# Down projection of two ConvFFNs: a chunk's norm is issued inside the next chunk

## Chip, cores and metric

The kernel runs on one core of one Trainium2 chip. The metric is device time in microseconds, the median of the runs. All times below come from the runs, from one profiled execution, or are worked out from its rows.

## The reference, cut to what matters

Two layers, each a mixer and a ConvFFN, on 1040 tokens (16 learned ones and 1024 given ones) of width 1024. Each sub-layer is wrapped in two RMS norms:

```
for i in range(2):
    h = h + rms_norm(mixer_i(rms_norm(h, pre)), post)
    h = h + rms_norm(conv_ffn(rms_norm(h, f_pre), w_up, c_w, c_b, w_down), f_post)
return h[:, 16:]

def conv_ffn(u, w_up, conv_w, conv_b, w_down):       # w_up 1024 x 5632, w_down 2816 x 1024
    h = causal_dwconv(u @ w_up, conv_w, conv_b)      # 3 taps
    g, up = split(h, 2)
    return (gelu(g) * up) @ w_down
```

The mixer of layer 0 is a gated linear recurrence beside a sliding-window attention, that of layer 1 a chunked state-space scan; both end in an output projection (2048 x 1024).

## The kernel before

Activations lie transposed, with the feature on the partitions and the tokens along the free dimension, in three chunks of tokens (348, 346 and 346 columns in layer 0; 342 each in layer 1, the first one of the last ConvFFN cut to 340). A product of two float32 values is made of three float32r matmuls: each operand is split into a high part (a ScalarE copy that rounds) and a low part (VectorE: value minus high part), and `mm3` issues high x high, high x low and low x high (L236, L237, L238).

**Weights.** `Weights` keeps one list of all weight tiles of the program in order of use. SyncE loads a tile of 128x1024 into `wst` (3 buffers), ScalarE and VectorE split it (`whi` L107, `wlo` L108) into two of the 8 buffers `w8`, so that at most four split tiles are alive. `get` hands out the next tile and issues the splits of the two after it.

**Down projection** (second half of `ffn`). For each chunk: load the 22 tiles of the gated product from DRAM (`mr`, L475) through the shared buffers `hc` (7 of them), split them into `mh` (L478) and `ml` (L479); then two halves `mb` of four output tiles each, and within a half 11 weight tiles. A weight tile serves two of the 22 tiles and four outputs, 24 matmuls. The four outputs of a half end together, go from PSUM to `yc` (L494, one buffer for the chunk) and are squared (`SqSum.add`). There are 6 PSUM banks for outputs, and 2 (`pb`) for the norms. Then the chunk's norm follows.

**Norm** (`norm_chunk`). It loads 8 tiles of the old `h` into `hc`. GpSimd has added up the 8 squares; 6 small matmuls (`pst`, L166) sum over the partitions, VectorE adds epsilon, GpSimd raises to -1/2, 6 small matmuls (`rb`, L180) spread the result over the partitions. Then for each of 8 tiles: VectorE multiplies `yc` by the norm's weight and by `rb` (`pt`, L205), GpSimd (VectorE for tiles 0 and 4, and for all in the last sub-layer) adds it to `h` (L207), and in layer 0's ConvFFN ScalarE and VectorE write the high and low part of the next sub-layer's input (L216, L217). Squares for the next norm are added up likewise.

**Up projection.** After three plain tiles the rest is multiplied by a seven-product scheme on halves of each operand. Its right-hand factors T1, T2, T4 (`right_factors`) and T3 (`third_factor`) are made once per layer from tiles `b` loaded from DRAM; T3 overwrites a part of `uh`/`ul` that the plain tiles read before. The subtractions of T2, T4 and T3 (L375, L377, L384) are GpSimd's, that of T1 is VectorE's. `right_factors` takes six `hc` buffers for each of its 8 steps. Results leave PSUM through `xs` (L334).

**Order.** The framework orders each engine's instructions when the program is built, by a simulated time line (`schedule_with_timeline_sim=True`): an engine takes the instruction that stands first in the program among those that are ready in that time line. On the chip each engine then follows that order.

The functions are printed with the profile's line numbers:

Of the kernel before, what the change touches and what calls it, by code (L numbers as in the profile page):

```python
# [13 lines left out]
F32 = mybir.dt.float32  # L14
# [125 lines left out]
class SqSum:  # L140
# [3 lines left out]
    def __init__(self, k, n, name):  # L144
        self.k, self.n, self.name, self.acc = k, n, name, None

    def add(self, src, m):
        k, nc, n = self.k, self.k.nc, self.n
        if self.acc is not None:
# [4 lines left out]
        if sq is not self.acc:  # L154
# [30 lines left out]
def norm_chunk(k, c, acc, y_of, h_src, h_dst, w_post, w_pre, name, between=lambda m: None, u_dst=None,  # L185
               more=None):
# [13 lines left out]
    if w_pre is not None:  # L200
        acc2 = SqSum(k, n, "h" + name)
    for m in range(NK):
        if y_of is not None:
            t = k.work.tile([P, NMAX], F32, tag="pt", bufs=2, name=f"pt_{name}_{m}")
            nc.vector.scalar_tensor_tensor(t[:, :n], y_of(m), w_post[:, m:m + 1], rb[:, :n], ALU.mult, ALU.mult)  # L205
            eng = nc.vector if m % 4 == 0 or w_pre is None else nc.gpsimd
            eng.tensor_tensor(h[m][:, :n], h[m][:, :n], t[:, :n], ALU.add)  # L207
        if h_dst is not None:
            nc.sync.dma_start(h_dst(m, t0, n), h[m][:, :n])
        if w_pre is None:  # L210
            continue
        if u_dst is not None:
            acc2.add(h[m][:, :n], m)
            continue
        hi, lo = k.uh[:, m, t0:t0 + n], k.ul[:, m, t0:t0 + n]
        nc.scalar.activation(hi, h[m][:, :n], AF.Copy, scale=w_pre[:, m:m + 1])  # L216
        nc.vector.scalar_tensor_tensor(lo, h[m][:, :n], w_pre[:, m:m + 1], hi.bitcast(F32), ALU.mult, ALU.subtract)  # L217
        if y_of is not None or m >= 4:
            for j in (range(m + 1) if y_of is None and m == 4 else (m,)):
                acc2.add(h[j][:, :n], j)  # L220
# [69 lines left out]
def ffn(k, W, lay, chunks, out_lo, conv_w, conv_b, ud, md, norm):  # L290
# [7 lines left out]
    with ExitStack() as es:  # L298
# [62 lines left out]
        def quarter(nm, s, kk):  # L361
            t0, n, _ = HALF[lay][s]
            b = k.work.tile([P, NMAX], F32, tag="hc", bufs=7, name=f"{nm}_{lay}_{s}_{kk}")[:, :n]
# [101 lines left out]
    with ExitStack() as es:  # L465
        ypool = es.enter_context(tc.tile_pool(name=f"ffy{lay}", bufs=1, reuse_waits="tile"))
        pool = es.enter_context(tc.tile_pool(name=f"ffd{lay}", bufs=1, side="right", reuse_waits="tile"))
        pp = es.enter_context(tc.tile_pool(name=f"ffdps{lay}", bufs=6, space=PSUM, reuse_waits="tile"))
        for ci, (t0, n) in enumerate(chunks):
            o = max(out_lo - t0, 0)  # L470
            t0, n = t0 + o, n - o
            mid = []
            for i in range(NFF):
                r = k.work.tile([P, NMAX], F32, tag="hc", bufs=7, name=f"mr{lay}_{ci}_{i}")
                nc.sync.dma_start(r[:, :n], md[i][:, t0:t0 + n])  # L475
                h = pool.tile([P, NMAX], F32R, tag="mh", bufs=NFF, name=f"mh{lay}_{ci}_{i}")
                l = pool.tile([P, NMAX], F32R, tag="ml", bufs=NFF, name=f"ml{lay}_{ci}_{i}")
                nc.scalar.copy(h[:, :n], r[:, :n])  # L478
                nc.vector.tensor_tensor(l[:, :n], r[:, :n], h[:, :n].bitcast(F32), ALU.subtract)  # L479
                mid.append((h, l))  # L480
            yc = ypool.tile([P, NK, NMAX], F32, tag="yc", bufs=1, name=f"fy{lay}_{ci}")
            acc = SqSum(k, n, f"y{lay}_{ci}")
            for mb in (0, 1):
                ps = [pp.tile([P, 512], F32, tag="ps", name=f"dn{lay}_{ci}_{mb}_{q}") for q in range(4)]
                for i in range(NFF):
                    if i % 2 == 0:
                        w = W.get("dn", lay, ci, mb, i // 2)
                    h, l = mid[i]
                    for q in range(4):
                        s = slice((i % 2) * 512 + q * P, (i % 2) * 512 + (q + 1) * P)  # L490
                        mm3(nc, ps[q][:, :n], w[0][:, s], w[1][:, s], h[:, :n], l[:, :n], i == 0, i == NFF - 1)
                for q in range(4):
                    m = mb * 4 + q
                    nc.scalar.copy(yc[:, m, :n], ps[q][:, :n])  # L494
                    acc.add(yc[:, m, :n], m)
            norm((t0, n), acc, lambda m: yc[:, m, :n], f"f{lay}_{ci}")
# [38 lines left out]
def out_proj(k, W, zd, chunks, norm, lay):  # L535
# [5 lines left out]
    with ExitStack() as es:  # L541
# [4 lines left out]
        for ci, (t0, n) in enumerate(chunks):  # L546
# [10 lines left out]
            acc = SqSum(k, n, f"o{lay}_{ci}")  # L557
# [27 lines left out]
            norm((t0, n), acc, lambda m: yc[:, m, :n], f"o{lay}_{ci}", (pool, "zr", 4))  # L585
# [656 lines left out]
def build(tc, I, O):  # L1242
# [16 lines left out]
    with ExitStack() as es:  # L1259
# [29 lines left out]
        def norm(s):  # L1289
            def f(c, acc, y_of, name, more=None):  # L1290
# [5 lines left out]
                           u_dst=None if s % 2 else lambda m, t0, n: ud[m][:, t0:t0 + n], more=more)  # L1296
# [40 lines left out]
```

## Time and profile before

| what | value |
|---|---|
| median of 3 runs | 3317.67 us (3315.75 to 3318.92) |
| the profiled execution's own time | 3317.06 us |
| its span, first to last instruction | 3315.3 us |
| outside the span | 1.8 us |
| TensorE busy | 3160.7 us, 95% |
| mean granted TensorE clock | 0.976 |

TensorE is busy for most of the span, so what counts is where it is not, and where it runs at the lower of its two clock levels (granted clock 0.50).

### The profile page before, as it was taken

How to read it: one execution, taken by the hardware profiler on the slowest of the kernel's cores; microseconds unless marked ns; L12 is line 12 of the kernel's file. 1: busy time of each engine (PE TensorE's matmuls, PEld its weight loads, DVE VectorE, ACT ScalarE, POOL GpSimd, SP SyncE). 2: the span in 40 equal slices, each digit the busy share in tenths (PEclk: the TensorE clock that was granted, in tenths of full speed). 3: DMA queues.
4: the chain of work that ended last, by engine and by line, in shares of the span. 5: the costliest groups of instructions: out<-in, count | busy, mean ns of one | idle time of the engine just before them, and what ended most of it. 6: DMA issues, size and time to landing. Idle time of an engine off the chain costs nothing.

```text
span 3315.3 us, 55448 instructions
## 1 busy us (share of the span) xinstructions
PE 3160.7 (95%) x21424; PEld 3046.8 (92%) x21424; DVE 2114.8 (64%) x3877; ACT 1609.7 (49%) x2920; POOL 539.7 (16%) x902
## 2 busy tenths in 40 slices
PE   8999999999999998989999999999999999999888
PEld 8888887999999998989999999999999999999888
DVE  6654344556888873455786667765565888885443
ACT  6763455554544453444554444444454544544332
POOL 3110000335000001123121111111244400000000
PEclk9999999999999999989999999999999999999889
DMA  3211013664222244553111111111575422225553
GB/s 127 80 64 59 29 36 115 202 222 138 88 84 78 78 159 138 185 181 99 37 44 45 37 50 53 41 43 45 193 225 175 125 81 82 81 83 183 188 172 106
DMA packets 165481, 352.59 MB, mean 106 GB/s; under 512 B 20032, under 2 KB 99808, under 8 KB 165216
## 3 DMA queue, kind: packets, MB, share of 16 engines
q1 hardware_dynamic: 165216, 349.04, 32.4%
q8 instruction: 168, 2.75, 0.3%
q14 instruction: 97, 0.79, 0.1%
HBM read 282.78 MB, written 65.59 MB: 105 GB/s over the span
## 4 chain that ended last, share of the span: by engine, by line
PE 83%; DVE 4%; ACT 4%; DMA 3%; issue 3%; POOL 2%; SPq 0%; POOLq 0%; DVEq 0%; ACTq 0%
PE ps_g L236 6%; PE ps_g L238 6%; PE ps_g L237 6%; PE upS L236 5%; PE upS L237 5%; PE upS L238 5%; PE dn L237 5%; PE dn L238 5%; PE dn L236 5%; PE op L238 2%; PE op L237 2%; PE op L236 2%; PE upA L236 2%; DMA zr<-zd 2%; PE upA L237 2%
## 5 line engine op out<-in xcount | busy, mean ns | idle before, releaser
L108 DVE TENSOR_TENSOR wlo<-wst,whi 128x1024 fp32r<-128x1024 f32 x318 | 394.7, 1244 | 401.3 <-ACT whi L107 383.4
L107 ACT CAST whi<-wst 128x1024 fp32r<-128x1024 f32 x319 | 332.9, 1046 | 460.6 <-PE dn L237 234.8
L238 PE MATMUL ps_g<-uh,wlo 128*128 128x346 f32 (+2 forms) x1344 | 442.3, 329 | 0.6 <-DVE wlo L108 0.6
L236 PE MATMUL ps_g<-uh,whi 128*128 128x346 f32 (+2 forms) x1344 | 440.3, 328 | 0.6 <-DVE dtr L945 0.4
L237 PE MATMUL ps_g<-ul,whi 128*128 128x346 f32 (+2 forms) x1344 | 440.2, 328 | 0.0
L236 PE MATMUL dn<-mh,whi 128*128 128x346 f32 (+3 forms) x1056 | 339.0, 329 | 47.3 <-ACT mh L478 47.3
L237 PE MATMUL dn<-ml,whi 128*128 128x346 f32 (+3 forms) x1056 | 344.6, 326 | 2.9 <-DVE ml L479 2.9
L238 PE MATMUL dn<-mh,wlo 128*128 128x346 f32 (+3 forms) x1056 | 342.3, 325 | 0.0
L236 PEld LDWEIGHTS ps_g<-uh,whi 128*128 128x128 f32 x1344 | 253.8, 189 | 6.1 <-DVE dtr L945 0.7
L238 PEld LDWEIGHTS ps_g<-uh,wlo 128*128 128x128 f32 x1344 | 253.8, 189 | 5.3 <-DVE wlo L108 1.1
L237 PEld LDWEIGHTS ps_g<-ul,whi 128*128 128x128 f32 x1344 | 253.8, 189 | 4.2 <-issue 0.2
L238 PE MATMUL op<-zh,wlo 128*128 128x342 f32 (+2 forms) x768 | 248.6, 324 | 2.5 <-DVE wlo L108 2.3
L237 PE MATMUL op<-zl,whi 128*128 128x342 f32 (+2 forms) x768 | 249.6, 326 | 0.9 <-DVE zl L555 0.9
L236 PE MATMUL op<-zh,whi 128*128 128x342 f32 (+2 forms) x768 | 244.9, 326 | 4.5 <-ACT zh L554 4.0
L236 PEld LDWEIGHTS dn<-mh,whi 128*128 128x128 f32 x1056 | 203.0, 194 | 48.8 <-ACT mh L478 48.8
L237 PEld LDWEIGHTS dn<-ml,whi 128*128 128x128 f32 x1056 | 203.3, 193 | 4.7 <-DVE ml L479 4.7
L238 PEld LDWEIGHTS dn<-mh,wlo 128*128 128x128 f32 x1056 | 203.5, 193 | 0.0
L82 ACT CAST wb<-wst 128x512 fp32r<-128x512 f32 x228 | 141.0, 618 | 102.2 <-PE upS L238 94.1
L83 DVE TENSOR_TENSOR wb<-wst,wb 128x512 fp32r<-128x512 f32 x228 | 156.2, 686 | 25.6 <-ACT wb L82 25.6
L236 PE MATMUL upA<-uh,wb 128*128 128x260 f32 (+2 forms) x608 | 171.8, 283 | 0.0
L236 PE MATMUL upS<-uh,wb 128*128 128x260 f32 (+2 forms) x608 | 171.6, 282 | 0.0
L237 PE MATMUL upA<-ul,wb 128*128 128x260 f32 (+2 forms) x608 | 171.3, 282 | 0.0
(430 smaller groups left out, 8693.7 us busy)
## 6 DMA issues: line engine op xcount, KB each, us to landing
wst<-in_dn SPq DMA_DIRECT2D x132, 512.0 KB, 3.5
wst<-in_wo SPq DMA_DIRECT2D x96, 512.0 KB, 3.9
wst<-in_up SPq DMA_DIRECT2D x88, 512.0 KB, 3.5
wst<-in_w SPq DMA_DIRECT2D x74, 512.0 KB, 3.5
md<-cv_u SPq DMA_DIRECT2D x38, 260.0 KB, 2.1
zd<-x SPq DMA_DIRECT2D x16, 513.0 KB, 3.5
zr<-zd SPq DMA_DIRECT2D x48, 171.0 KB, 3.2
mr<-md SPq DMA_DIRECT2D x44, 173.0 KB, 3.3
```

What stands on the lines that cost most here:

```text
L82: nc.scalar.copy(p[:, 0], src)
L83: tt(p[:, 1], src, p[:, 0].bitcast(F32), ALU.subtract)
L107: nc.scalar.copy(h, s)
L108: nc.vector.tensor_tensor(l, s, h.bitcast(F32), ALU.subtract)
L236: nc.tensor.matmul(ps, lhsT=wh, rhs=xh, start=start, stop=False, skip_group_check=more)
L237: nc.tensor.matmul(ps, lhsT=wh, rhs=xl, start=False, stop=False, skip_group_check=more)
L238: nc.tensor.matmul(ps, lhsT=wl, rhs=xh, start=False, stop=stop, skip_group_check=more)
```

## The change

The norm of a chunk of the down projection is kept as a closure (`before`) and issued after the first half `mb` of the next chunk; the last chunk's norm follows after the loop. The split tiles (`mid`, high and low part in one tile) move from a pool on the right side of SBUF to the pool that holds `yc`, on the left side, where the factors T1, T2 and T4 of the up projection lay before; there are still 22. In each half the last weight tile is used output by output, so that the four outputs end one after the other.

For the last chunk of every sub-layer (`tail`, `last`) the squares are not added up by GpSimd: each square goes straight into 6 small matmuls that accumulate over the 8 tiles (`direct`). There, six of the eight additions to `h` are VectorE's and two GpSimd's (tiles 2 and 5).

In the up projection the subtractions of T2, T4 and T3 move from GpSimd to VectorE, and three of the six buffers of a step are taken from the norms' buffers `acc`, `sq` and `pt` in place of `hc`.

```diff
+    def __init__(self, k, n, name, direct=False):
+        self.first = True
+        if direct:
+            self.pst = k.pb.tile([P, 512], F32, tag="pb", name=f"pst_{name}")
     def add(self, src, m):
         nc.scalar.activation(sq[:, :n], src, AF.Square)
+        if self.direct:
+            nb, w, st = token_blocks(n)
+            for j in range(nb):
+                nc.tensor.matmul(self.pst[:w, j:j + 1], lhsT=sq[:, st[j]:st[j] + w], rhs=k.mean_d, start=self.first,
+                                 stop=m == NK - 1, skip_group_check=True)
+                self.first = False
     def rsqrt(self, name):
+        if self.direct:
+            return rsqrt_rows(self.k, self.pst, self.n, name)
...
+            if last:
+                eng = nc.gpsimd if m in (2, 5) else nc.vector
+            else:
+                eng = nc.vector if m % 4 == 0 or w_pre is None else nc.gpsimd
...
+            tag, bufs = {"b21": ("acc", 2), "t1": ("sq", 2), "t2": ("pt", 2)}.get(nm, ("hc", 7))
...
-                nc.gpsimd.tensor_tensor(t2, b22, t1, ALU.subtract)
+                nc.vector.tensor_tensor(t2, b22, t1, ALU.subtract)
-                nc.gpsimd.tensor_tensor(b21, b21, t2, ALU.subtract)
+                nc.vector.tensor_tensor(b21, b21, t2, ALU.subtract)
...
-                nc.gpsimd.tensor_tensor(b12, b22, b12, ALU.subtract)
+                nc.vector.tensor_tensor(b12, b22, b12, ALU.subtract)
...
-        pool = es.enter_context(tc.tile_pool(name=f"ffd{lay}", bufs=1, side="right", reuse_waits="tile"))
+        before = None
+            tail = ci == len(chunks) - 1
-                h = pool.tile([P, NMAX], F32R, tag="mh", bufs=NFF, name=f"mh{lay}_{ci}_{i}")
-                l = pool.tile([P, NMAX], F32R, tag="ml", bufs=NFF, name=f"ml{lay}_{ci}_{i}")
+                x = ypool.tile([P, 2, NMAX], F32R, tag="mid", bufs=NFF, name=f"mid{lay}_{ci}_{i}")
+                h, l = x[:, 0, :n], x[:, 1, :n]
...
+            def part(m, js):
+                for i in js:
+                    w = ws[i // 2]
+                    s = slice((i % 2) * 512 + m % 4 * P, (i % 2) * 512 + (m % 4 + 1) * P)
+                    mm3(nc, ps[m][:, :n], w[0][:, s], w[1][:, s], *mid[i], i == 0, i == NFF - 1)
+            for mb in (0, 1):
+                ms = range(mb * 4, mb * 4 + 4)
+                for m in ms:
+                    ps[m] = pp.tile([P, 512], F32, tag="ps", name=f"dn{lay}_{ci}_{m}")
+                for i in range(0, NFF - 2, 2):
+                    ws[i // 2] = W.get("dn", lay, ci, mb, i // 2)
+                    for m in ms:
+                        part(m, (i, i + 1))
+                ws[NFF // 2 - 1] = W.get("dn", lay, ci, mb, NFF // 2 - 1)
+                for m in ms:
+                    part(m, (NFF - 2, NFF - 1))
+                if mb == 0:
+                    if before:
+                        before()
+                    yc = ypool.tile([P, NK, NMAX], F32, tag="yc", bufs=1, name=f"fy{lay}_{ci}")
+                    acc = SqSum(k, n, f"y{lay}_{ci}", tail)
+                for m in ms:
+                    nc.scalar.copy(yc[:, m, :n], ps[m][:, :n])
+                    acc.add(yc[:, m, :n], m)
-            norm((t0, n), acc, lambda m: yc[:, m, :n], f"f{lay}_{ci}")
+            def before(c=(t0, n), acc=acc, yc=yc, name=f"f{lay}_{ci}", tail=tail):
+                norm(c, acc, lambda m: yc[:, m, :c[1]], name, tail=tail)
+        before()
...
+            tail = ci == len(chunks) - 1
+            acc = SqSum(k, n, f"o{lay}_{ci}", tail)
```

The last two lines stand in `out_proj`, which passes `tail` on to its norm as well.

## Rows read from the trace of the kernel before

**Rows 1.** Page: busy us (share of the span) and instructions of each engine.
```profile
PE 3160.7 (95%) x21424; PEld 3046.8 (92%) x21424; DVE 2114.8 (64%) x3877; ACT 1609.7 (49%) x2920; POOL 539.7 (16%) x902
```

**Rows 2.** Waits of TensorE: who waited for whom, us in total, times, longest.
```profile
PE dn L236 <- ACT mh L478: 47.3, 6, 9.3
PE pst_post_f L166 <- POOL acc_y L155: 23.4, 5, 4.9
PE upS L236 <- ACT xs L334: 14.3, 2, 7.5
PE ps_up L236 <- ACT xs L334: 9.9, 2, 5.0
```

**Rows 3.** Windows: us from start, length, busy (count) per engine, PEclk, DMA share, GB/s.
```profile
1214.40:1226.90 12.50, 5.42 (x18) 4.95 (x18) 10.75 (x19) 6.23 (x13) 0.00 (x0) 0.59 0.55 164
1308.40:1332.70 24.30, 9.21 (x32) 8.41 (x33) 16.64 (x24) 12.43 (x28) 17.31 (x17) 0.58 0.50 153
1345.00:1409.00 64.00, 64.00 (x402) 64.00 (x401) 22.22 (x21) 22.62 (x29) 3.04 (x3) 1.00 0.51 164
1415.50:1438.50 23.00, 7.90 (x29) 7.07 (x29) 15.28 (x22) 11.41 (x25) 17.25 (x16) 0.55 0.49 152
...
3089.50:3111.00 21.50, 7.03 (x27) 6.62 (x27) 10.36 (x21) 4.12 (x9) 4.93 (x5) 0.60 0.53 160
3192.50:3216.80 24.30, 9.01 (x33) 8.65 (x34) 11.13 (x23) 5.24 (x12) 4.95 (x5) 0.58 0.50 153
767.90:779.70 11.80, 5.63 (x23) 5.43 (x23) 8.60 (x19) 7.39 (x18) 2.71 (x9) 0.71 0.58 177
...
827.50:837.80 10.30, 3.57 (x16) 3.58 (x17) 7.88 (x14) 6.19 (x16) 4.24 (x9) 0.67 0.38 119
...
777.00:823.00 46.00, 46.00 (x284) 46.00 (x283) 41.56 (x77) 29.45 (x63) 29.53 (x41) 0.97 0.50 150
```

**Rows 4.** Time line of TensorE, last norm of layer 0's output projection: start, us.
```profile
747.53 0.67 PE L166 MATMUL pst_post_o<-mean_d,acc_o 128*116 128x1 f32 x6
...
752.29 0.82 PE L180 MATMUL rb_post_o<-ident,rr_post_o 116*128 116x116 f32 x6
```

**Rows 5.** Time line of VectorE in three norms: start, us, [idle before, releaser].
```profile
753.15 1.06 DVE L205 SCALAR_TENSOR_TENSOR pt_o<-yc,vec,rb_post_o 128x346 f32<-128x346 f32 x2 [4.74 <-PE rb_post_o L180]
...
1317.42 1.06 DVE L205 SCALAR_TENSOR_TENSOR pt_f<-fy,vec,rb_post_f 128x348 f32<-128x348 f32 x2 [2.66 <-PE rb_post_f L180]
...
1326.67 0.56 DVE L205 SCALAR_TENSOR_TENSOR pt_f<-fy,vec,rb_post_f 128x348 f32<-128x348 f32 x1
...
3098.55 1.04 DVE L205 SCALAR_TENSOR_TENSOR pt_f<-fy,vec,rb_post_f 128x340 f32<-128x340 f32 x2 [2.66 <-PE rb_post_f L180]
...
3103.97 1.04 DVE L205 SCALAR_TENSOR_TENSOR pt_f<-fy,vec,rb_post_f 128x340 f32<-128x340 f32 x2
```

**Rows 6.** The line L494 alone: ns min/median/max, first and last start, forms.
```profile
L494 ACT COPY fy<-dn x48: 434/447/461, 1265.0 to 3297.7; 128x346 f32<-128x346 f32 x16, 128x342 f32<-128x342 f32 x16, 128x348 f32<-128x348 f32 x8, 128x340 f32<-128x340 f32 x8
```

**Rows 7.** The line L107, 1240 to 1300 us: ScalarE idle before it until, us, times.
```profile
  PE dn L237: 39.7, 15
```

**Rows 8.** Time line of TensorE: one sum of squares within dense matmuls.
```profile
1337.21 0.68 PE L166 MATMUL pst_pre_f<-mean_d,acc_hf 128*116 128x1 f32 x6
1337.75 0.40 PE L236 MATMUL dn<-mh,whi 128*128 128x346 f32 x1
1338.00 0.32 PE L237 MATMUL dn<-ml,whi 128*128 128x346 f32 x1
```

**Rows 9.** Time line of ScalarE at layer 0's first seven-product tile.
```profile
831.40 0.41 ACT L358 CAST uh<-b 128x260 fp32r<-128x260 f32 x1 [2.85 <-POOL b L384]
...
833.73 0.45 ACT L334 COPY xs<-ps_up_2u 128x348 f32<-128x348 f32 x1
```

**Rows 10.** The line L375 alone: ns min/median/max.
```profile
L375 POOL TENSOR_TENSOR t<-b,t x16: 737/1085/3109, 778.0 to 2599.9; 128x260 f32<-128x260 f32 x8, 128x258 f32<-128x258 f32 x4, 128x256 f32<-128x256 f32 x4
```

**Rows 11.** The line L359, 777 to 820 us: ns min/median/max.
```profile
L359 DVE TENSOR_TENSOR T1l<-t,T1h x8: 414/556/974, 778.3 to 816.2; 128x260 fp32r<-128x260 f32 x8
```

More of the change, by code (lines that the diff above doesn't have):

```diff
@@ L140 @@
 class SqSum:
-    def __init__(self, k, n, name):
-        self.k, self.n, self.name, self.acc = k, n, name, None
+    def __init__(self, k, n, name, direct=False):
+        self.k, self.n, self.name, self.acc, self.direct = k, n, name, None, direct
+        self.first = True
+        if direct:
+            self.pst = k.pb.tile([P, 512], F32, tag="pb", name=f"pst_{name}")
     def add(self, src, m):
         k, nc, n = self.k, self.k.nc, self.n
-        if self.acc is not None:
+        if self.acc is not None or self.direct:
             sq = k.work.tile([P, NMAX], F32, tag="sq", bufs=2, name=f"sq_{self.name}_{m}")
@@ L153, in add @@
         nc.scalar.activation(sq[:, :n], src, AF.Square)
-        if sq is not self.acc:
+        if self.direct:
[4 more added lines that the diff above has]
+                self.first = False
+        elif sq is not self.acc:
             nc.gpsimd.tensor_tensor(self.acc[:, :n], self.acc[:, :n], sq[:, :n], ALU.add)
     def rsqrt(self, name):
+        if self.direct:
+            return rsqrt_rows(self.k, self.pst, self.n, name)
         return token_rsqrt(self.k, self.acc, self.k.mean_d, self.n, name)
@@ L185, in norm_chunk @@
 def norm_chunk(k, c, acc, y_of, h_src, h_dst, w_post, w_pre, name, between=lambda m: None, u_dst=None,
-               more=None):
+               more=None, last=False):
     nc = k.nc
@@ L200, in norm_chunk @@
     if w_pre is not None:
-        acc2 = SqSum(k, n, "h" + name)
+        acc2 = SqSum(k, n, "h" + name, last)
     for m in range(NK):
@@ L362, in quarter @@
             t0, n, _ = HALF[lay][s]
-            b = k.work.tile([P, NMAX], F32, tag="hc", bufs=7, name=f"{nm}_{lay}_{s}_{kk}")[:, :n]
+            tag, bufs = {"b21": ("acc", 2), "t1": ("sq", 2), "t2": ("pt", 2)}.get(nm, ("hc", 7))
+            b = k.work.tile([P, NMAX], F32, tag=tag, bufs=bufs, name=f"{nm}_{lay}_{s}_{kk}")[:, :n]
             if nm[0] == "b":
@@ L480, in ffn @@
+                h, l = x[:, 0, :n], x[:, 1, :n]
+                nc.scalar.copy(h, r[:, :n])
+                nc.vector.tensor_tensor(l, r[:, :n], h.bitcast(F32), ALU.subtract)
                 mid.append((h, l))
-            yc = ypool.tile([P, NK, NMAX], F32, tag="yc", bufs=1, name=f"fy{lay}_{ci}")
-            acc = SqSum(k, n, f"y{lay}_{ci}")
-            for mb in (0, 1):
[L484 to L494, printed above, removed]
+            ps, ws = {}, {}
@@ L556, in out_proj @@
             yc = ypool.tile([P, NK, NMAX], F32, tag="yc", bufs=1, name=f"yc{lay}_{ci}")
-            acc = SqSum(k, n, f"o{lay}_{ci}")
+            tail = ci == len(chunks) - 1
+            acc = SqSum(k, n, f"o{lay}_{ci}", tail)
             ps = {}
@@ L584, in out_proj @@
                 done(m)
-            norm((t0, n), acc, lambda m: yc[:, m, :n], f"o{lay}_{ci}", (pool, "zr", 4))
+            norm((t0, n), acc, lambda m: yc[:, m, :n], f"o{lay}_{ci}", (pool, "zr", 4), tail)
 def mixer0_lru(k, W, V, zd, tail):
@@ L1289, in norm, with f @@
         def norm(s):
-            def f(c, acc, y_of, name, more=None):
+            def f(c, acc, y_of, name, more=None, tail=False):
                 last = s == upto - 1
@@ L1295, in f @@
                            nw(2 * s + 1), None if last else nw(2 * s + 2), name,
-                           u_dst=None if s % 2 else lambda m, t0, n: ud[m][:, t0:t0 + n], more=more)
+                           u_dst=None if s % 2 else lambda m, t0, n: ud[m][:, t0:t0 + n], more=more, last=tail)
             return f
```

3 lines of the change are left out of this document (removed).

## The prediction, made before the changed kernel ran

> **What bounds the kernel now.** The page comes first: TensorE is busy 95% of the span and no other compute engine more than 64% [rows 1], so only a stretch in which TensorE waits or runs at the low clock level can give time back. The list of its waits says where: six times, 47.3 us in all, before the down projection's first matmul of a chunk, 23.4 us before the sum over the partitions in the norms, 14.3 and 9.9 us in the up projection for results that ScalarE has not yet taken out of PSUM [rows 2]. The windows then price each place with its clock. In dense down-projection work a matmul starts every 64.0/402 = 0.16 us at a granted clock of 1.00; in the windows around the holes the mean granted clock is 0.55 to 0.71, as the matmuls go on at the low level (1.2 GHz) for some us after a hole [rows 3]. What a window loses is its length, less 0.16 us for each large matmul in it, less 1.4 us where a norm's two sets of 6 small matmuls lie in it (0.63, worked out below, and 0.8 for `rb`), since these stay. That gives:
> - before a layer's down projection: 12.5 - 18 x 0.16 = 9.6 us, twice 19.2 (layer 1 taken as layer 0);
> - between chunks, four times: 24.3 - 1.4 - 20 x 0.16 = 19.7; 23.0 - 1.4 - 17 x 0.16 = 18.9; 21.5 - 1.4 - 15 x 0.16 = 17.7; 24.3 - 1.4 - 21 x 0.16 = 19.5; in all 75.8 us;
> - after an output projection (only `rb` in the window): 11.8 - 0.8 - 17 x 0.16 = 8.3, twice 16.6;
> - at the first seven-product tile, where a matmul has 260 columns, 0.16 x 260/346 = 0.12: 10.3 - 16 x 0.12 = 8.4, twice 16.8.
>
> Together 128 us: the most that the change can win back there.
>
> **The norm inside the next chunk.** Today ScalarE and VectorE do a chunk's norm ahead of the next chunk's splits, and the norm's `h` tiles hold `hc`, so TensorE has nothing to do. With the norm later in the program, the next chunk's 22 tiles are loaded and split during the half before, as each slot falls free, and TensorE goes straight on. The hole moves. The norm now stands behind the next chunk's first half, and TensorE, which has a ready matmul all through that half, comes to it when the half ends (call this T). `yc` has one buffer, so ScalarE's copies of that half's four outputs wait until the norm has read its last `yc` tile; queued behind them on ScalarE are squares and splits for which there is no room yet; and TensorE waits for them, since of 6 banks only two are free for the second half.
>
> How long: from `pst` to the first `pt` 753.15 - 747.53 = 5.6 us pass where TensorE has other work in between [rows 4, 5]. From the first `pt` to the end of the eighth it takes 1326.67 + 0.56 - 1317.42 = 9.8 us in layer 0 and 3103.97 + 1.04 - 3098.55 = 6.5 in layer 1 [rows 5]. A copy out of PSUM takes 0.45 [rows 6], with 0.1 for its signals. So a third bank is free at T + 15.95 or T + 12.65. The cover: in dense stretches ScalarE starts a split only when TensorE releases a weight tile [rows 7], so the four tiles of `w8` are all there is; with two banks they give 4 x 12 matmuls x 0.16 = 7.7 us, and with the norm's small ones 9.1. TensorE stands 6.9 us in layer 0, 3.5 in layer 1. Clock: the window before the down projection has 12.5 - 5.42 = 7.1 us without a matmul and loses 9.6, so 2.5 go to the clock; I add 2.5 to the 6.9 and 2.0 to the 3.5. What stays is 2 x 9.4 + 2 x 5.5 = 29.8 of 75.8: saved 46.0. Bounds: 75.8 if the cover lasts, and about 0 if nothing covers and the splits come late too; I take the middle, as each duration has its row.
>
> The norm's 8 loads and 8 stores move on SyncE's queue as well, behind the 22 loads of the next chunk, which need the same `hc`; they have the first half (11 weight tiles x 24 x 0.16 = 42 us) for it, and the stores that wait for the additions hold up weight loads only for the norm's 10 us, less than the three tiles in `wst` last (11.5). Cost nothing; with that cover gone, the rest of those 10 us. GpSimd's queue has nothing else there.
>
> **The splits' new place.** Today `mh` lies where the up projection's `xs` and `cv` lay, and waits for the last of these (9.6 us, twice). The new place is that of T1, T2 and T4; behind T1's last use come four products of 24 matmuls, 4 x 24 x 0.12 = 11.5 us, in which the first splits can be made. VectorE is busy 10.75 of 12.5 us around that place [rows 3], so its low parts may be late: I leave 2 us each and save 15.2; bounds 0 and 19.2.
>
> **Squares into TensorE.** 6 small matmuls lie between 1337.21 and 1337.75, and the next start comes 0.25 later in place of 0.16: 0.63 us a group [rows 8]. A tail sum has 8 groups in place of one, 7 x 0.63 = 4.4 us more. There are seven such sums: for the post-norm and the following pre-norm in both output projections and in layer 0's ConvFFN, and for the post-norm at the end. The four in the output projections cost 17.6 and shorten the norm (no addition of squares on GpSimd, most additions to `h` on VectorE), so that results leave PSUM before TensorE has filled its banks: 16.6 saved. The two in layer 0's ConvFFN cost 8.8 and buy nothing, as no wait of rows 2 lies there. The one at the end costs 4.4; of its wait (23.4/5 = 4.7 [rows 2]) a copy, a square and a group stay, 1.6, and two additions fewer on VectorE give 0.5 or so: net +1.0. Bounds for a group: 0 inside a hole, and 0.63 with a wait of its own. Together 17.6 - 16.6 + 8.8 + 1.0 = +10.8. A bank of `pb` held by these sums leaves the norm before with one, for `pst` and `rb` in turn: nothing, as they follow each other anyway.
>
> **Factors.** At the first seven-product tile ScalarE's copy out of PSUM (833.73) stands behind casts of T3 that wait for GpSimd's subtractions, one until 831.40 [rows 9]. With more `hc` free the loads come earlier, and a subtraction of 0.74 to 3.1 us on GpSimd [rows 10] becomes about 0.41 on VectorE, as the shortest L359 [rows 11]. Per layer 24 move: 24 x 0.41 = 10 us onto VectorE, which is busy 41.56 of 46 us there [rows 3], so 4.4 are free. Two things ease that: its rows run long beside GpSimd's (414 to 974 ns for one form [rows 11]), and some of its work may come later. I take 11 of the 16.8 as saved; bounds 16.8 saved and 2 x 5.6 = 11 lost.
>
> The Trainium skill (SBUF — State Buffer, Who interferes with whom) has a sharper rule for this: a VectorE instruction with two SBUF inputs and a GpSimd one that reads SBUF keep each other out for a whole instruction. The trace agrees in kind (the same subtraction took 737 or 3109 ns [rows 10]), yet only part of VectorE's rows is long. By the rule VectorE could win back more than it takes on, and the sum would be 5.8 lower.
>
> **Sum.** -46.0 - 15.2 + 10.8 - 11 = -61.4 on the profiled execution's 3317.06: 3256 us. The median of the runs lies 0.6 above it, which changes nothing.
>
> **Rivals.**
> - *The norm is covered* (0.20): the build's order brings `pst` forward into the first half, or finds more to put into the hole. For it: the order fills each engine with what is ready. Against: the dense stretch has no idle TensorE to fill [rows 3]. 29.8 less: 3226.
> - *Nothing covers* (0.17): the second half's matmuls on the two free banks are not drawn ahead of those that wait for a bank. Holes of 15.95 - 1.4 = 14.6 and 11.2, with 2.5 each for the clock: 2 x 17.1 + 2 x 13.7 = 61.6 in place of 29.8: 3288.
> - *VectorE becomes the bound of the factor stage* (0.06): 11 lost in place of 11 saved: 3278. Its busy share speaks for it, the rows that run long beside GpSimd's against.
> - *Slower: the squares hold TensorE's queue* (0.06). 7 x 8 = 56 groups stand among dense matmuls, each behind a copy and a square on ScalarE. If the order gives each its turn too early by the length of these, some 0.45 + 0.45 with signals and ScalarE's own queue 1.25 us, TensorE loses 56 x 1.25 = 70: 3326; from 61.4/56 = 1.10 us a group it decides. Against: where `rb` waits for a chain of two engines, the order put 4.8 us of other matmuls ahead of it [rows 4], so it leaves room. The Trainium skill (TensorE: Matmul & The Clock Gate, The mechanism) says that matmuls start and end strictly in program order, which this rival needs; no row of before shows a dense stretch held so.
>
> **Numbers.** My forecast has 0.51, with 3237 to 3277 as its own range (2 us either way per hole, and the factors). The whole range, 3220 to 3292, takes in the covered and the uncovered norm and leaves out the slower side. About 0.2% of the time, 6.6 us, is what a measurement can tell from no change. Faster by more 0.90, within it 0.04, slower by more 0.06.
>
> **What would show it.** In the profile after: no hole before a layer's first down-projection matmul and none between chunks; four holes of 3 to 7 us in mid-chunk, each ended by ScalarE's copy from PSUM to `yc`, with a granted clock of 0.50 behind them; 56 groups of 6 small matmuls among dense ones; the wait at the first seven-product tile shorter, that after the output projections gone. It would be wrong if the mid-chunk holes are absent or above 12 us, if a norm's `pst` stands within a first half, if TensorE waits for squares, or if VectorE has no idle time left in the factor stage.

## The result, and the profile after

The changed kernel takes 3281.52 us (median of 4 runs, 3280.35 to 3281.77) against 3316.71 (4 runs, 3314.26 to 3318.92): a ratio of 0.9893, 95% interval 0.9876 to 0.9911. That is 35.2 us less, a gain clear of the noise and of the sign that was forecast, but little more than half of the 61.4 us that the sum gave. The profiled execution took 3280.35 us, its span is 3278.5, the mean granted clock 0.984.

The page's first part, beside [rows 1]: TensorE has 294 more instructions, 49 more groups of 6 small matmuls (seven sums with 8 groups in place of one), and GpSimd 107 fewer.

```profile
PE 3181.2 (97%) x21718; PEld 3071.6 (94%) x21718; DVE 2113.0 (64%) x3935; ACT 1606.2 (49%) x2920; POOL 467.8 (14%) x795
```

The waits of TensorE after (who waited for whom, us in total, times, longest), beside [rows 2]:

```profile
PE dn L251 <- ACT fy L524: 21.3, 4, 6.9
PE dn L251 <- ACT mid L495: 12.4, 2, 6.2
PE ps_up L251 <- ACT xs L349: 9.9, 2, 5.0
...
PE pst_hf L161 <- ACT sq_hf L156: 4.0, 3, 2.6
```

The six waits for splits are down to the two at a layer's start, four new ones stand in mid-chunk, the waits behind the output projections are unchanged to the tenth, TensorE now waits for squares, and those for `xs` at the seven-product tiles and for GpSimd's sum (`acc_y`) are gone. The windows after (us from start, length, busy and count of each engine, PEclk, DMA share, GB/s), beside [rows 3]:

```profile
1212.00:1230.00 18.00, 10.91 (x49) 10.25 (x49) 14.36 (x27) 10.83 (x22) 0.00 (x0) 0.72 0.60 191
1359.00:1376.00 17.00, 10.07 (x52) 9.82 (x51) 12.07 (x16) 12.31 (x28) 15.65 (x14) 0.80 0.58 168
1367.00:1371.00 4.00, 4.00 (x16) 4.00 (x15) 1.42 (x2) 2.96 (x8) 3.43 (x5) 0.50 0.63 179
...
1502.00:1546.00 44.00, 40.03 (x245) 38.61 (x244) 22.90 (x44) 14.52 (x30) 6.66 (x15) 0.84 0.20 61
784.00:830.00 46.00, 46.00 (x281) 46.00 (x281) 43.42 (x103) 30.52 (x68) 26.92 (x27) 0.96 0.61 180
```

First the start of the down projection, as sparse as before. Then the first mid-chunk hole, and the matmuls right behind it: 16 in 4.0 us, at the low level. The fourth row is new: behind layer 0's down projection, where the kernel before had no hole, TensorE is idle for 4 us and at a mean clock of 0.84.

A cut of the time lines at the start of the first or last matmul of each kind shows where the time went. The columns are: from the output projection's first matmul to the first seven-product tile (both layers added); the seven-product tiles (both); last up-projection to first down-projection matmul (both); first to last matmul of the down projection, layer 0 and layer 1; from there to the 201st matmul of mixer 1's large products; from layer 1's last to the end; the span. All from the profiled executions, in us.

| kernel | to seven-product | seven-product | start | down 0 | down 1 | behind 0 | end | span |
|---|---|---|---|---|---|---|---|---|
| before | 558.6 | 779.8 | 13.3 | 301.2 | 293.6 | 45.6 | 18.4 | 3315.3 |
| after | 571.5 | 762.0 | 13.0 | 282.5 | 268.3 | 60.1 | 16.4 | 3278.5 |
| sums on GpSimd | 556.9 | 762.0 | 13.0 | 280.2 | 267.5 | 59.8 | 17.2 | 3263.7 |
| four buffers | 567.9 | 762.1 | 13.0 | 284.2 | 271.4 | 62.6 | 15.9 | 3281.7 |
| factors alone | 560.3 | 763.0 | 13.0 | 303.1 | 293.0 | 45.6 | 19.0 | 3299.6 |
| down alone | 555.8 | 781.7 | 13.0 | 278.1 | 266.7 | 58.2 | 16.9 | 3275.3 |
| norm in first half | 572.5 | 762.0 | 13.0 | 269.2 | 257.2 | 59.6 | 16.1 | 3254.7 |
| yc in two halves | 571.9 | 762.0 | 13.0 | 268.8 | 258.5 | 60.4 | 16.7 | 3256.2 |
| early splits | 573.3 | 762.7 | 0.2 | 277.9 | 265.1 | 60.0 | 16.0 | 3260.4 |
| two pools | 572.2 | 762.0 | 13.0 | 281.9 | 268.5 | 50.3 | 16.3 | 3267.2 |
| first splits left | 570.9 | 762.0 | 3.7 | 277.9 | 265.6 | 50.0 | 16.3 | 3251.2 |
| yc low | 572.3 | 762.0 | 13.0 | 282.3 | 269.9 | 60.1 | 16.1 | 3279.0 |
| together | 558.4 | 762.2 | 0.2 | 260.8 | 250.6 | 45.4 | 16.9 | 3198.9 |

After against before: the down projections give 18.7 + 25.3 = 44.0, the seven-product tiles 17.8, the end 2.0; the way to the seven-product tiles takes back 12.9 and the stretch behind layer 0's down projection 14.5. What is left, 0.3 at the starts, makes the span's 36.7. The two mixers ahead of the output projections are in no column but the span: the first of them took 543.9 to 548.4 us in these executions, though no edit touches it. So a difference of 2 or 3 us between two executions is not yet an effect of an edit.

### The profile page after: what moved, and what is told of

It is laid out like the page before. It is cut to its first block, busy times and chain, and to the rows that moved or that the text cites. A ratio compares the mean times of both kernels' runs of the same rounds, so it can differ in the third digit from the quotient of the medians.

```text
span 3278.5 us, 56016 instructions
## 1 busy us (share of the span) xinstructions
PE 3181.2 (97%) x21718; PEld 3071.6 (94%) x21718; DVE 2113.0 (64%) x3935; ACT 1606.2 (49%) x2920; POOL 467.8 (14%) x795
## 4 chain that ended last, share of the span: by engine, by line
PE 82%; issue 6%; ACT 4%; DVE 3%; DMA 3%; POOL 1%; SPq 0%; DVEq 0%; POOLq 0%; ACTq 0%
PE ps_g L251 6%; PE ps_g L253 6%; PE ps_g L252 6%; PE upS L251 5%; PE upS L252 5%; PE upS L253 5%; PE dn L252 4%; PE dn L253 4%; PE dn L251 4%; DMA zr<-zd 3%; PE upA L251 2%; PE upA L252 2%; PE upA L253 2%; PE op L253 2%; PE op L252 2%
## 5 line engine op out<-in xcount | busy, mean ns | idle before, releaser
L107 ACT CAST whi<-wst 128x1024 fp32r<-128x1024 f32 x319 | 332.4, 1046 | 415.5 <-PE dn L252 162.0
L251 PE MATMUL dn<-mid,whi 128*128 128x346 f32 (+3 forms) x1056 | 344.0, 328 | 33.7 <-ACT fy L524 21.3
L252 PE MATMUL dn<-mid,whi 128*128 128x346 f32 (+3 forms) x1056 | 343.8, 326 | 1.7 <-DVE mid L496 1.7
L253 PE MATMUL dn<-mid,wlo 128*128 128x346 f32 (+3 forms) x1056 | 342.1, 326 | 0.0
L251 PEld LDWEIGHTS dn<-mid,whi 128*128 128x128 f32 x1056 | 204.1, 194 | 35.3 <-ACT fy L524 22.4
L252 PEld LDWEIGHTS dn<-mid,whi 128*128 128x128 f32 x1056 | 203.9, 193 | 2.6 <-DVE mid L496 2.6
L253 PEld LDWEIGHTS dn<-mid,wlo 128*128 128x128 f32 x1056 | 203.4, 193 | 0.0
```

Of the source, the lines that this page charges most:

```text
L107: nc.scalar.copy(h, s)
L251: nc.tensor.matmul(ps, lhsT=wh, rhs=xh, start=start, stop=False, skip_group_check=more)
L252: nc.tensor.matmul(ps, lhsT=wh, rhs=xl, start=False, stop=False, skip_group_check=more)
L253: nc.tensor.matmul(ps, lhsT=wl, rhs=xh, start=False, stop=stop, skip_group_check=more)
```

## The experiments

Each run has the kernel before beside it on the same chip (medians 3316.1, 3318.4, 3318.0 and 3316.7 in the four groups); ratios are to that.

### The sums of squares

**Sums back on GpSimd** in the changed kernel:

```diff
-        acc2 = SqSum(k, n, "h" + name, last)
+        acc2 = SqSum(k, n, "h" + name)
...
-                    acc = SqSum(k, n, f"y{lay}_{ci}", tail)
+                    acc = SqSum(k, n, f"y{lay}_{ci}")
...
-            acc = SqSum(k, n, f"o{lay}_{ci}", tail)
+            acc = SqSum(k, n, f"o{lay}_{ci}")
```

> The changed kernel (3281.5) with every sum of squares back on GpSimd; the additions to h in the last norms stay on VectorE as in the change. Theory A: the groups on TensorE are what ate the gain. In the trace after, the way from the output projection's first matmul to the first seven-product tile is longer than before by 7.3 us in layer 0 and 5.6 us in layer 1, the stretch behind layer 0's down projection by 14.5, and the end is shorter by 2.1; all of that goes back: 3281.5 - 12.9 - 14.5 + 2.1 = 3256. Theory B: the groups fill time that TensorE has anyway, and the loss came from the additions' new engines or from the norm's new place: the time stays within 6 us of 3281.5.

Measured: 3264.02 us, ratio 0.9842 (0.9827 to 0.9856), 17.5 us better than the change. A is right for the output projections: 571.5 falls to 556.9, below the 558.6 of before. It is wrong behind layer 0's down projection: 59.8 stays, and the waits now name another cause.

```profile
PE dn L251 <- ACT fy L524: 21.3, 4, 6.9
PE ps_g L251 <- DVE dtr L979: 13.9, 1, 13.9
PE dn L251 <- ACT mid L495: 12.4, 2, 6.2
PE ps_up L251 <- ACT xs L349: 9.9, 2, 5.0
```

Mixer 1's first large products (`ps_g`) wait 13.9 us for VectorE to take `dtr` out of PSUM. In the change the groups for the squares, and the 4.0 us of waits for them, fill the same time.

**Four buffers for the squares:**

```diff
-            sq = k.work.tile([P, NMAX], F32, tag="sq", bufs=2, ...
+            sq = k.work.tile([P, NMAX], F32, tag="acc" if self.direct and m % 2 else "sq", bufs=2, ...
```

> The changed kernel, with the squares that go straight to TensorE in four buffers in place of two (odd ones in the two buffers of the running sum, which such a norm doesn't use). Theory A: the last norms are paced by two buffers; each pair of squares waits until TensorE has come to the pair before, some 19 matmuls further on. With four, layer 0's last rb of the output projection comes 5 us or more sooner, the 5.0 us stalls behind both output projections go with 3 us of low clock each, and of the 4 us of waits for squares behind layer 0's down projection 3 go: 3281.5 - 16 - 3 = 3262. Theory B: the place in TensorE's order sets the pace whatever the buffers, or the groups' own 0.63 us are the loss: within 4 us of 3281.5, and the stalls of 5.0 us stand.

Measured: 3278.56 us, ratio 0.9884 (0.9868 to 0.9901). Both theories are half right. Two buffers did set the pace, as the time lines of the changed kernel show; first TensorE's groups of two tiles (12 matmuls) among the up projection's matmuls, 4.2 to 4.3 us apart:

```profile
761.08 1.28 PE L161 MATMUL pst_ho<-mean_d,sq_ho 128*116 128x1 f32 x12
...
765.34 1.28 PE L161 MATMUL pst_ho<-mean_d,sq_ho 128*116 128x1 f32 x12
...
769.55 1.28 PE L161 MATMUL pst_ho<-mean_d,sq_ho 128*116 128x1 f32 x12
```

and ScalarE's squares, each pair waiting for the group before it:

```profile
761.87 1.07 ACT L156 ACTIVATE sq_ho<-h_o 128x346 f32<-128x346 f32 x2 [3.48 <-PE pst_ho L161]
766.10 0.49 ACT L156 ACTIVATE sq_ho<-h_o 128x346 f32<-128x346 f32 x1 [3.16 <-PE pst_ho L161]
766.74 0.49 ACT L156 ACTIVATE sq_ho<-h_o 128x346 f32<-128x346 f32 x1
770.31 1.10 ACT L156 ACTIVATE sq_ho<-h_o 128x346 f32<-128x346 f32 x2 [3.08 <-PE pst_ho L161]
```

With four buffers both 5.0 us stalls behind the output projections are gone from the waits. The time hardly moves all the same: the median is 3.0 us lower, and the intervals of the two ratios overlap. The way to the seven-product tiles is 280.9 us in layer 0 and 287.1 in layer 1, 567.9 with the digits kept: 3.5 less than with two buffers and still 9.3 more than before. (The profiled execution, at 3283.76 us the slowest of the four, took 7.3 us longer than the change in the down projections and behind layer 0's.)

The stalls themselves were 9.9 us in all; the low clock that was to go with them stayed. In both kernels the clock stands at 0.50 for 6.8 us in layer 0 and for 10.2 in layer 1. First the two windows with two buffers, then the two with four:

```profile
780.60:787.40 6.80, 5.23 (x18) 5.23 (x19) 5.44 (x14) 4.44 (x12) 3.56 (x6) 0.50 0.90 255
2555.50:2565.70 10.20, 5.83 (x20) 5.83 (x21) 9.06 (x23) 7.92 (x19) 2.03 (x13) 0.50 0.80 248
```

```profile
766.90:773.70 6.80, 6.80 (x29) 6.80 (x30) 0.16 (x1) 0.00 (x0) 1.01 (x5) 0.50 0.16 42
2545.30:2555.50 10.20, 10.20 (x45) 10.20 (x45) 0.16 (x1) 0.60 (x2) 1.06 (x3) 0.50 0.21 63
```

With four buffers TensorE works through the whole of both, at the low level. So from the output projection's last matmul on 8.2 us are saved in the two layers, not 16.6; and 4.7 are lost ahead of it, in layer 0 with a wait of 1.2 us for a square, in layer 1 with waits in the output projection, most of them for `zh`, which the edit does not touch. Two sums with 7 groups more each, at 0.63 us, are 8.8 us a layer, and what they could take away was a stall of 5.0 us: the trade does not pay.

### The parts by themselves

**Factors alone**, the kernel before with the three lines of subtractions and the line of tags from the diff ahead of the prediction:

> The kernel before (3316.7) with the factor part of the change alone: the subtractions on VectorE and three of the six factor tiles out of the hc buffers. Theory A: this part saves what the stage shows in the trace after (from the first seven-product tile to the last up-projection matmul 8.6 us less in layer 0 and 9.2 in layer 1), and it does so by itself: 3316.7 - 17.8 = 3299. Theory B: it needs the rest of the change (the last norm ending elsewhere moves the stage's start): a saving under 8 us, 3309 or more.

Measured: 3301.52 us, ratio 0.9952 (0.9938 to 0.9967). A: 16.8 us less in the seven-product tiles, 14.6 in the median.

**Engine alone**, the subtractions on VectorE and the tags as before:

```diff
-                nc.gpsimd.tensor_tensor(t2, b22, t1, ALU.subtract)
+                nc.vector.tensor_tensor(t2, b22, t1, ALU.subtract)
```

(the same for `b21` in `right_factors` and `b12` in `third_factor`)

> The kernel before (3316.1) with the subtractions of the factor stage on VectorE, and nothing else; all six factor tiles stay in the hc buffers. Theory A: GpSimd's slow subtractions (0.74 to 3.1 us) were what the casts waited for: at least 12 of the 14.6 us that the whole factor part saves, 3304 or less. Theory B: the hc buffers were, through late loads: less than 5 us, 3311 or more.

Measured: 3300.70 us, ratio 0.9946 (0.9931 to 0.9961), as much as the whole part; the tags do nothing that shows. The line of T1's low part, VectorE's own before and after (ns min/median/max), took 414/556/974 in [rows 11]; here:

```profile
L359 DVE TENSOR_TENSOR T1l<-t,T1h x8: 417/432/446, 779.0 to 814.9; 128x260 fp32r<-128x260 f32 x8
```

**Down projection alone**, the kernel before with the change's second half of `ffn`, without `tail`:

> The kernel before with the down-projection part of the change alone (norm inside the next chunk, splits in a pool of their own), sums of squares and factors as before. Theory A: the parts add up. The down projections took 18.7 and 25.3 us less in the trace after, the place before their first matmul the same: 3316.7 - 44 = 3273, with mid-chunk holes of 6.9 and 3.7 us. Theory B: part of the 44 us came from the sums on TensorE, which end a norm sooner: 3285 or more.

Measured: 3276.94 us, ratio 0.988 (0.9866 to 0.9895). The mid-chunk holes are those of the change, and the 11 us hole behind layer 0's down projection is there without any sum on TensorE, so it belongs to this part:

```profile
PE dn L236 <- ACT fy L508: 21.3, 4, 6.9
...
PE ps_g L236 <- DVE dtr L962: 11.0, 1, 11.0
```

The parts add up: 3316.1 - 14.6 - 39.2 = 3262.3 against 3264.0 with the sums on GpSimd; the sums on TensorE are the 17.5 between that and the change. Two details of the change had no run of their own: the additions to `h` in the last norms on other engines, for which these sums leave 1.7 us, within the noise, and the last weight tile used output by output, which is part of the down projection alone.

### The mid-chunk holes

**Norm ahead of the first half:**

```diff
+            if before:
+                before()
             for mb in (0, 1):
...
                 if mb == 0:
-                    if before:
-                        before()
                     yc = ypool.tile(...
```

> The changed kernel (3281.5) with a chunk's norm issued ahead of the next chunk's first half in place of behind it. Theory A: the four mid-chunk holes (6.9, 6.9, 3.7, 3.8 us, each with 3 to 7 us of low clock behind it) come from yc alone, which is read too late for the next chunk's copies; with the norm's reads done in the first 20 us of a half that takes 42, all four go, about 10 us each in layer 0 and 6 in layer 1: 3281.5 - 32 = 3250. Theory B: the norm's work then stands ahead of what the first half needs (loads, splits, the sums on TensorE), and new holes at the starts of the chunks take their place: 3272 or more.

Measured: 3256.42 us, ratio 0.9812 (0.9796 to 0.9829). A: the line of `fy` is gone from the waits; the down projections take 13.3 and 11.1 us less, 24.5 of the 32 with the digits kept. In layer 0 two short waits for the following norm's sum stand instead:

```profile
PE pst_pre_f L178 <- POOL acc_hf L165: 3.6, 2, 2.2
```

**yc in two halves**, the norm where the change has it:

```diff
-                    yc = ypool.tile([P, NK, NMAX], F32, tag="yc", bufs=1, name=f"fy{lay}_{ci}")
+                    yc = [ypool.tile([P, 4, NMAX], F32, tag=f"yc{q}", bufs=1, ...) for q in (0, 1)]
```

> The changed kernel (3281.5) with yc as two tiles of four outputs each in place of one of eight; the norm stays behind the next chunk's first half. Theory A: the copies out of PSUM wait for the norm's reads of yc and for nothing else. The first half's four copies then wait for four of the eight reads only, 4.9 us less in layer 0 and 3.3 in layer 1: holes of 2.0 and 0.4 us in place of 6.9 and 3.7, a saving of 16 with no change of the clock's share, up to 22 with it: 3260 to 3265. Theory B: ScalarE is late for other reasons (the norm's own casts and squares stand ahead of the copies in its order): holes of 5 us or more in layer 0 stay, 3275 or more.

Measured: 3257.35 us, ratio 0.9817 (0.9802 to 0.9832). A, and a little more: no wait for `fy` is left among the larger ones, the down projections take 13.7 and 9.9 us less, and waits for a weight's low part stand there instead:

```profile
PE dn L253 <- DVE wlo L108: 4.3, 3, 2.2
```

So what the copies waited for was the reads of `yc`. The changed kernel's line L524 says the same: ScalarE stood idle before these copies until the norm's last `pt`.

```profile
L524 ACT COPY fy<-dn x48: 431/447/481, 1263.4 to 3262.5; 128x346 f32<-128x346 f32 x16, 128x342 f32<-128x342 f32 x16, 128x348 f32<-128x348 f32 x8, 128x340 f32<-128x340 f32 x8
its engine sat idle before it (us, times) until:
  DVE pt_f L217: 25.0, 4
```

### The start of the down projection, and what comes behind it

ScalarE's time line in the changed kernel shows why the hole at the start stayed: the first splits' casts stand behind the last tile's last activations, and these wait for VectorE.

```profile
1213.50 0.81 ACT L321 ACTIVATE cv_g<-xs_g,vec 128x520 f32<-128x520 f32 x1
1217.50 0.64 ACT L340 ACTIVATE cv_g<-cv_g 128x520 f32<-128x520 f32 x1 [3.20 <-DVE cv_g L323]
1218.17 0.82 ACT L321 ACTIVATE cv_u<-xs_u,vec 128x520 f32<-128x520 f32 x1
1218.90 1.23 ACT L495 CAST mid<-mr 128x348 fp32r<-128x348 f32 x3
```

And VectorE's behind layer 0's down projection: the last norm's eight `pt` from 1511.69 on, then `dtr`, whose matmuls had ended by 1506:

```profile
1511.69 1.06 DVE L217 SCALAR_TENSOR_TENSOR pt_f<-fy,vec,rb_post_f 128x346 f32<-128x346 f32 x2 [3.16 <-PE rb_post_f L192]
...
1519.36 1.05 DVE L217 SCALAR_TENSOR_TENSOR pt_f<-fy,vec,rb_post_f 128x346 f32<-128x346 f32 x2
...
1522.16 0.51 DVE L979 TENSOR_TENSOR dtr<-dtp,rb 64x348 f32<-64x348 f32 x1
1522.59 0.50 DVE L537 TENSOR_TENSOR xs_s<-ps_g,rb 128x348 f32<-128x348 f32 x1
```

**Early splits.** T1 moves into a pool that outlives the up projection; the first six splits of a chunk live in it:

```diff
+    def split_low(ci, i, t0, n):
+        return split(ci, i, t0, n, *(x.rearrange("p a b -> p (a b)")[:, i * NMAX:i * NMAX + n] for x in M))
...
             both("S1", "T1", C, True, after_p5)
+            if i == NFF - 1:
+                split_early()
...
+            mid = early if ci == 0 else [split_low(ci, i, t0, n) for i in range(NE)]
+            for i in range(NE, NFF):
```

> The changed kernel with the first six splits of each chunk kept in the place of T1, in a pool of its own that outlives the up projection; for the first chunk they are loaded and cast right behind the last tile's third product, the last that reads T1. Theory A: the hole of 6.2 us before a layer's first down-projection matmul stands because the casts are ordered behind the last activations of the up projection, nothing else; with the casts earlier, 12 x 12 matmuls have their data, and the hole goes with its low clock: 2 x 8 less, 3265. Theory B: VectorE is too full there (14.4 of 18 us busy), the low parts come late whatever the order: holes above 3 us stay, 3274 or more.

Measured: 3260.17 us, ratio 0.9825 (0.981 to 0.984). A: the start goes from 13.0 us to 0.2 in all, and the window runs at a clock of 1.00 where the change had 0.72; 21.4 us in place of 16. VectorE is busier than before and not late:

```profile
1212.00:1230.00 18.00, 17.77 (x117) 17.48 (x116) 15.49 (x26) 11.19 (x18) 0.18 (x1) 1.00 0.68 218
```

**Two pools**, the splits on the right-hand side as before, `yc` alone on the left:

```diff
+        pool = es.enter_context(tc.tile_pool(name=f"ffd{lay}", bufs=1, side="right", reuse_waits="tile"))
...
-                x = ypool.tile([P, 2, NMAX], F32R, tag="mid", bufs=NFF, ...
+                x = pool.tile([P, 2, NMAX], F32R, tag="mid", bufs=NFF, ...
```

> The changed kernel with the splits in a pool on the right-hand side, as before, and yc alone in the left-hand one; all else as in the change. Theory A: behind layer 0's down projection the first copies of mixer 1 out of PSUM (dtr, xs) are ordered behind the whole last norm, because their tiles lie where the pool lay that also holds yc; TensorE runs out of banks meanwhile. With yc elsewhere they come first, and of the 14.5 us that this stretch got longer about 11 go (the sums on TensorE keep some 3): 3270. Theory B: the squares that TensorE waits for there are the cause, and they stay: 3278 or more.

Measured: 3272.22 us, ratio 0.9859 (0.9844 to 0.9873). A: `dtr` comes right behind its matmuls, ahead of the norm, and the stretch falls from 60.1 to 50.3.

```profile
1501.41 0.51 DVE L980 TENSOR_TENSOR dtr<-dtp,rb 64x348 f32<-64x348 f32 x1 [0.37 <-PE dtp L979]
1504.28 0.16 DVE L186 TENSOR_SCALAR rs_post_f<-pst_y 116x3 f32<-116x3 f32 x1 [2.36 <-PE pst_y L161]
```

**First splits left.** No line moves; only the place in memory changes:

```diff
-                x = ypool.tile([P, 2, NMAX], F32R, tag="mid", bufs=NFF, ...
+                mp, bufs = (ypool, 12) if i < 12 else (pool, NFF - 12)
+                x = mp.tile([P, 2, NMAX], F32R, tag="mid", bufs=bufs, ...
```

> The changed kernel with yc and the first 12 splits of a chunk in the left-hand pool, over T1, T2 and T4 only, and the other 10 in a right-hand pool; no line moves in the program. Theory A: place in memory alone sets both orders. The first splits' casts come ahead of the last tile's last two activations, so the holes of 6.2 us before the down projections shrink below 3 us (6 us a layer with the clock), and the stretch behind layer 0's down projection gets its 9.3 us back as with two pools: 3281.5 - 12 - 9 = 3260. Theory B: for the start of the down projection the place in the program counted (the early splits also moved their lines): holes of 5 us or more stay, 3270 or more.

Measured: 3254.09 us, ratio 0.9809 (0.9794 to 0.9823). A, by more than expected: the start is 3.7 in place of 13.0, and the stretch behind 50.0. The casts now stand behind the first of the three activations shown above, not behind the last:

```profile
1213.34 0.81 ACT L321 ACTIVATE cv_g<-xs_g,vec 128x520 f32<-128x520 f32 x1
1214.05 2.77 ACT L497 CAST mid<-mr 128x348 fp32r<-128x348 f32 x7
```

**yc low in the common pool:**

```diff
+            if ci == 0:
+                yc = ypool.tile([P, NK, NMAX], F32, tag="yc", bufs=1, name=f"fy{lay}_{ci}")
             mid = []
```

> The changed kernel with yc allocated ahead of the splits in their common pool, so that it lies at the pool's low end, where no tile of mixer 1's first products lies over it; the splits take the rest, in the same pool. Theory A: what puts mixer 1's first copies (dtr, xs) behind the last norm is that yc shares a pool with tiles that they overlie, not that they overlie yc itself: they stay behind it, and the time within 4 us of 3281.5. Theory B: the overlap itself counts: they come first as with two pools, 3272.

Measured: 3279.22 us, ratio 0.9883 (0.9867 to 0.99). A: `dtr` stays behind the last `pt`:

```profile
1517.96 1.05 DVE L217 SCALAR_TENSOR_TENSOR pt_f<-fy,vec,rb_post_f 128x346 f32<-128x346 f32 x2
...
1520.77 0.50 DVE L982 TENSOR_TENSOR dtr<-dtp,rb 64x348 f32<-64x348 f32 x1
```

Which pool `yc` shares decides the order, not which bytes it takes. That the framework, in its simulated time line, lets a tile wait for all of a pool that it overlies fits all three runs, but is not shown by itself.

**Together:** sums on GpSimd, norm ahead of the first half, early splits, and splits 6 to 11 on the left with `yc`, 12 to 21 on the right:

> Four edits of these runs on the changed kernel together: sums of squares back on GpSimd, norm ahead of the next chunk's first half, first six splits early in T1's place, and the other splits in two pools so that yc does not lie under mixer 1's first tiles. Theory A: the losses stand in different stretches and add up: 3264 - 25 (mid-chunk holes) - 21 (starts) - 14 (behind layer 0's down projection, 59.8 to 45.6) = 3204, against 3316 before. Theory B: they share a cover (the order pushes the same work from one hole to the next): 3225 or more.

Measured: 3200.48 us (3197.68 to 3202.29), ratio 0.9645 (0.9629 to 0.9661), 117.6 us better than before and 81.0 better than the change. A: the losses stand apart and add up. The largest of TensorE's waits that is left is the stall behind the output projections; in the down projections it is the norms' sums:

```profile
PE ps_up L251 <- ACT xs L371: 9.9, 2, 5.0
...
PE pst_pre_f L178 <- POOL acc_hf L165: 3.7, 2, 2.2
```

## Why the prediction was right or wrong

The sum gave 3256 us, and 3281.5 came: inside the whole range of 3220 to 3292, but above the forecast's own, 3237 to 3277. Three of its own signs came out against it: the holes before a layer's first down-projection matmul stood, so did the waits after the output projections, and TensorE waited for squares.

The run with the sums on GpSimd splits the spans' 36.7 us: against before it stands at -47.1 in the down projections, -17.8 in the factors' stage, +14.2 behind layer 0's down projection, -0.3 at the starts. The change adds 17.2 to that run: 14.6 up to the seven-product tiles, 3.1 in the down projections, 0.4 behind layer 0's, and 0.9 less at the end. The remaining -2.9 is what that run saves elsewhere, 1.7 on the way to the seven-product tiles and 1.2 at the end. These come to -36.7.

- **The norm inside the next chunk: right, in mechanism and size.** Forecast -46.0, measured -47.1 (-50.0 with the down part alone). The holes were worked out as 6.9 and 3.5 us and came as 6.93, 6.89, 3.73 and 3.76, ended by the copy to `yc`, with a clock of 0.50 behind them; none stands between chunks. The cover by two banks and four weight tiles was the right count: between `pst` and each hole the trace has 48 matmuls of the down projection, 4 x 12. What they still cost is 24.5 us by the run without them, where 29.8 were set.
- **The splits' new place: the step that failed.** Forecast -15.2; measured -0.3 at the starts and +14.2 behind layer 0's down projection, 29 us off and more than the whole miss of 24.7. (The other misses, +6.4, -6.8, -1.1 and -2.9, come to -4.4: that the first two all but cancel is luck.) The text said that the new place "is that of T1, T2 and T4". By the kernel's own sizes that can't hold: 22 x 2 x 348 x 4 + 8 x 348 x 4 bytes make 72.4 KB a partition, the six factor tiles 6 x 4 x 520 x 4, 49.9 KB. The pool also covers where `xs` and `cv` lay, so the casts stayed behind the last activations (first splits left: only place changed, and they came earlier). Of the first four splits the built program puts only the first on T1, and the next three on `xs`. (In the kernel before it was `ml` that lay on `xs` and `cv`; `mh`, of which the text says so, lay on the factors.) And the other end was not looked at: the pool with `yc` now lies under mixer 1's first tiles, so its first copies out of PSUM were ordered behind the last norm, which before were not (two pools). The step asked what the new place waits for, and not what will wait for the new place.
- **Squares into TensorE: failed in its second term.** Forecast +10.8, measured +17.2 (17.5 in the medians). The groups' own price was near, though its +1.0 for the end is 0.8 by its own terms: 14.6 in the output projections where 17.6 was set, 2.7 in layer 0's ConvFFN and behind it where 8.8 was set (part of them fell into the new hole), 0 at the end and in layer 1 where 1.0 was. The 16.6 saved did not come: the stalls of 5.0 us stood, since two buffers let the squares go only by pairs. With four they went, and 3.5 us came back, not 16.6: the price of 8.3 a stall counted the low clock in, and that stayed, 6.8 and 10.2 us at 0.50, though TensorE then had no hole there.
- **Factors: right, undersized.** Forecast -11 with bounds of -16.8 and +11; measured -17.8. Both waits for `xs` at the first seven-product tile are gone. The work that VectorE took on was set at 10 us in 46 with 4.4 free; it is busy 43.42, only 1.9 more than before, since its rows got shorter. In the change the new subtraction takes (ns min/median/max)

```profile
L391 DVE TENSOR_TENSOR t<-b,t x8: 421/424/432, 786.7 to 808.8; 128x260 f32<-128x260 f32 x8
```

  where GpSimd's took 737/1085/3109 [rows 10]. The term that was too small is what VectorE wins back. The Trainium skill (SBUF — State Buffer, Who interferes with whom) says that such a VectorE instruction and GpSimd's reads of SBUF shut each other out; the run with the engine alone agrees: T1's low part went from a median of 556 ns to 432 when only GpSimd's subtractions moved. By that rule the sum was to be 5.8 us lower; the stage came out 6.8 lower than forecast.
- **The rivals.** "Nothing covers" gave 3288, nearer to 3281.5 than the forecast, but by holes of 14.6 and 11.2 us that no row shows: a right number for a wrong reason. The norm was not covered by the build's own order, though it can be (norm ahead of the first half). VectorE did not become the bound. The squares did hold TensorE's queue, for 4.0 us in all, in one place, and not for 1.10 us a group.

## What to carry to other kernels

When tiles move to another pool, work out from their sizes what their whole pool overlies, and look at both ends: what the first of them waits for, and which tiles of the next stage will lie on them and so wait for their last reader. A sum that moves to the engine that is the bound must pay for itself even when it removes a stall; here 8.8 us of small matmuls a layer could buy a stall of 5.0 us, and the low clock behind it stayed. A buffer with one slot that a late reader holds shows up as a hole where the next writer comes, and half the buffer, or an earlier reader, closes it.

## What the runs showed of the hardware

A short hole need not bring the low level with it. With the first splits on the left TensorE stands 1.5 us before the down projection, and the window's granted clock stays at 1.00, where the hole of 6.2 us gave 0.72:

```profile
1212.00:1230.00 18.00, 15.48 (x98) 14.98 (x97) 16.29 (x29) 11.24 (x22) 0.00 (x0) 1.00 0.76 228
```

So taking 4.7 and 4.6 us off these two holes gave back another 4.6 us in layer 0's down projection and 2.8 in layer 1's, where the first matmuls no longer run at the low level.

Nor does the low level need a hole. With four buffers for the squares TensorE is busy without a pause from 750 to 773.7 us. There it does 48 small matmuls of one column with few large ones between, and in the midst of them the granted clock falls from 1.00 to 0.50:

```profile
762.23 1.28 PE L161 MATMUL pst_ho<-mean_d,sq_ho 128*116 128x1 f32 x12
...
763.62 1.28 PE L161 MATMUL pst_ho<-mean_d,sq_ho 128*116 128x1 f32 x12
...
765.80 1.31 PE L161 MATMUL pst_ho<-mean_d,sq_ho 128*116 128x1 f32 x12
...
767.41 2.34 PE L161 MATMUL pst_ho<-mean_d,sq_ho 128*116 128x1 f32 x12
```

The last of the four groups takes 2.34 us in place of 1.28, and the large matmuls behind it start every 0.29 us in place of 0.16. In layer 1 the clock falls in the same bunch, for 10.2 us. With two buffers the groups stand 4.2 to 4.3 us apart among dense matmuls, and the clock stays at 1.00 until the hole.
